# Fused matrix product, bias and tanh by Strassen-Winograd products: the last tanh of a pair written to a tile of the outputs' pool, and the leaving pair reading both m5 sums ahead of m6's products

## The chip, the cores and the metric

The kernel runs on one core of a Trainium2 chip. The metric is the device time of one execution in microseconds; lower is better. The kernel before took 1536.89 us, the median of three runs between 1536.08 and 1539.6 us. The engines are named as in the profile: PE does matrix products (PEld loads its weights beside it), DVE does elementwise work on two operands, ACT does tanh and copies, POOL and SP issue transfers here and compute nothing that matters.

## The reference

```python
def reference(a, b, bias):        # all float32; a, b 4096 x 4096, bias 4096
    return np.tanh(np.matmul(a, b) + bias)
```

## The kernel before

The product is cut in four columns `c` of 1024 output columns (two halves `j` of 512) and, in each, sixteen row pairs of 2 x 128 output rows. One item of work is one pair in one column. An item's 2 x 2 blocks are made by the Strassen-Winograd scheme: seven products `m1` to `m7` in place of eight, each of 16 matmuls of 128x128 weights against 128x512 data in float16. Their left operands are differences of quadrants of `a` (`s1`, `s2`, `s5`, `s6`, `s7`), their right operands sums of blocks of `b` (`d1`, `d3`, `d4`, `e6`, `e7`); DVE makes both. The products are summed in the eight PSUM banks (`ps`) and in float32 tiles: `ds` collects the first output row's left half (and gives the second row's left half on the way), `s` the first row's right half, `o` the second row's right half.

Columns 0 and 1 and the beginnings of columns 2 and 3 are ordinary items or items taken by two. The end of the single items of columns 2 and 3 is done by `four(n)`, which takes two items `p = n` and `q = n + 1` together and does some of their products by the same scheme a second time: `m4`, `m2` and `m3` in every pair, `m6` in all but the leaving one, and `m5` in those that are neither first nor leaving are computed for both items as seven half products of 8 matmuls of 128x256 each, in three groups. `group0` is the half products with left operands `s5` and `s2`, `group1` those with `s1`, `d3` and `d4`, `group2` those with `s7` and `s6`. The small left operands `h` are made by `left(...)` into four places that are used in turn; those right operands (`form`) that are not in SBUF are loaded again, 512 KB each, by POOL whenever a place comes free (`pull_four`). The third sum of a group goes through a copy `x` on ACT (`third`). Column 2 has four such pairs, column 3 has five. The fourth of column 2 is the leaving pair (`leave`), after which the next items are ordinary again; the fifth of column 3 is the last of the program.

The schedule is written by hand: every engine does its instructions in the order in which the code issues them, and tiles of a pool are handed out in turn. Three pools matter. `temps` has two buffers under the name `ds` and two under `sc` (the tile `s`). `outs` has three buffers under the name `o`. A buffer is written again only when the last reader of its earlier tile is done; where that reader is the store to DRAM, when the store has landed.

How a pair ends, and how the next begins, is what the change touches. The function `end` (L933) closes a tile: `tanh` on ACT over the tile itself, and the store by SP (L474) from it. The closing of `ds` and of one set of the tiles `s` is put into the list `left_over`, which the next pair empties a few at a time with `more(4)`, `more(3)`, `more(2)` and `more(1)` (L889) between its own half products, so that these tanhs lie beside `group0` and `group1` of the next pair's `m4` and `m2`. Behind `group2` of `m4` the next pair takes its own two `ds` tiles: `take_d(p)` and `take_d(q)` (L955), DVE additions of the bias to a bank. DVE does after that the operands `s5` and `s2` of the product `x`, which is `m6` in a steady pair. PE meanwhile does `group2` of `m2`, `group0` of `m3`, and then `group0` of `x`, which needs them.

In the leaving pair the order is `m1` of p and q, then for each item: `take("m5", i)` (DVE: two additions, then tanh and store of `s`), the whole product `m6`, `take("m6", i)`, the whole product `m7`, and the end of `ds`.

Of the kernel before, what the change touches and what calls it, by code (L numbers as in the profile page):

```python
# [23 lines left out]
TANH = mybir.ActivationFunctionType.Tanh  # L24
# [87 lines left out]
def kernel(  # L112
# [7 lines left out]
    nc = tc.nc  # L120
# [20 lines left out]
    def tt(out_, in0, in1, op):  # L141
        nc.vector.tensor_tensor(out=out_, in0=in0, in1=in1, op=op)  # L142
# [6 lines left out]
    def bank(n, s, what):  # L149
        two = items[n][2] is not None  # L150
        if what == "w":
            return banks[5 + 2 * (n % 2)]
        if what == "z":
            return banks[4 + 2 * (n % 2) + (s if two else 0)]
        return banks[(0 if what == "d" else 2) + (s if two else n % 2)]
# [158 lines left out]
    def asum(n, name, half=None):  # L314
        s = aset[n]
        x, y = {
            "s2": ("a21", "a22"), "s5": ("a12", "a11"), "s1": ("a22", "a11"),
            "s6": ("a21", "a11"), "s7": ("a22", "a12"),
        }[name]
        over = {"s6": "a21", "s7": "a12"}.get(name)  # L320
        if half == 1:
            pass
        elif name == "s6" and n in partner and by_two(n, "m6"):
            s[name] = side[:, :, ds(NB, NB)].rearrange("p a (b m) -> p a b m", m=P)
            tt(s[name], by_four(s[x]), by_four(s[y]), SUB)
            return
        elif over is None or stays(n):
            s[name] = new_sum([P, T, P], fp16, name, n)
        else:
            s[name] = s[over]  # L330
        ts_ = ds(0, T) if half is None else ds(half * TP, TP)
        tt(s[name][:, ts_], s[x][:, ts_], s[y][:, ts_], SUB)
# [140 lines left out]
    def store(o, pair, r, c, j):  # L473
        nc.sync.dma_start(  # L474
            out=out[ds((2 * pair + r) * P, P), ds(c * NCW + j * NB, NB)], in_=o
        )

    def new_out():
        return outs.tile([P, NB], fp32, name="o", tag="o")

    def result(src, *where):
        o = new_out()
        nc.scalar.activation(o, src, TANH)  # L483
        store(o, *where)
# [361 lines left out]
    def whole(n, left_, right, parts=None, anew=False):  # L846
        at = by_four(aset[n][left_])
        for to, half in parts or ((bank(n, 0, "z"), ds(0, NB)),):
            for t in range(T):
                nc.tensor.matmul(  # L850
                    to[:, half], at[:, t // TB, t % TB], bop[right, t // TB][:, t % TB, half],
                    start=anew and t == 0, stop=t == T - 1, skip_group_check=True,
                )
# [42 lines left out]
    def four(n):  # L896
        c = items[n][0]
        p, q, m = n, n + 1, n + 2
# [5 lines left out]
        pair = {i: items[i][1][0] for i in (p, q)}  # L904
        st = {i: state.setdefault((i, 0), {}) for i in (p, q)}
# [12 lines left out]
        def make(name, i):  # L918
            four_sum(i, name, home[name, i])
# [5 lines left out]
        def step(k):  # L925
            if leave:
                give_back(c, k)

        def one_whole(what, i):
            _, left_, right = next(v for v in PRODUCTS.values() if v[0] == what)  # L930
            whole(i, left_, right, ((bank(i, 0, mine.get(what, "z")), ds(0, NB)),), what in mine)

        def end(name, i, r, j):  # L933
            nc.scalar.activation(st[i][name], st[i][name], TANH)  # L934
            store(st[i][name], pair[i], r, c, j)

        def take(what, i, later=False):
            to = bank(i, 0, mine[what])
            if what == "m6":
                tt(st[i]["o"], st[i]["o"], to, ADD)  # L940
                ready = ("o", i, 1, 1)
            else:
                tt(st[i]["ds"], st[i]["ds"], to, SUB)
                tt(st[i]["s"], to, st[i]["s"], ADD)
                ready = ("s", i, 0, 1)
            if later:
                left_over.append(lambda: end(*ready))
            else:
                end(*ready)

        def take_c(i):
            st[i]["s"] = temps.tile([P, NB], fp32, name="s", tag="sc")
            tt(st[i]["s"], bank(i, 0, "c"), bias_bc[:, NB:], ADD)
# [5 lines left out]
        def take_z(i):  # L959
            st[i]["o"] = new_out()  # L960
            tt(st[i]["o"], st[i]["s"], bank(i, 0, "z"), SUB)
# [104 lines left out]
        if leave:  # L1066
            make("s1", q)
            make("s7", q)
            for i in (p, q):
                take_c(i)  # L1070
            one_whole("m1", p)
            step(12)
            take_z(p)
            one_whole("m1", q)
            take_z(q)
            step(13)
            for i in (p, q):
                take("m5", i)
                one_whole("m6", i)
                step(14 if i == p else 16)  # L1080
                take("m6", i)
                one_whole("m7", i)
                if i == p:
                    asum(m, "s2")
                tt(st[i]["ds"], st[i]["ds"], bank(i, 0, "z"), SUB)
                end("ds", i, 0, 0)
                step(15 if i == p else 17)
            asum(m, "s5")
            for k in range(18, 29):
                at_slot(SLOTS * m + k - 18, give_back, c, k)  # L1090
            return
# [247 lines left out]
    def at_slot(slot, f, *args):  # L1339
        work.setdefault(slot, []).append((f, args))  # L1340
# [403 lines left out]
    for slot in range(1 - len(ORDER), SLOTS * len(items)):  # L1744
        if slot in handed:
            if slot - 1 not in handed:
                c = max(c for c in FOURS if SLOTS * (begins[c] - 2) < slot)
                turn_over(c)
                for n in range(begins[c], ends_with[c], 2):
                    four(n)  # L1750
            continue
        for f, args in work.get(slot, ()):
            f(*args)
        if slot < 0:
            visit(slot + len(ORDER) - 1)
        elif slot == 3:
            last_visit(0)
            last_visit(1)
        for pos, p in PRODUCTS.items():
            n, r = divmod(slot - pos, SLOTS)  # L1760
            if r == 0 and n >= 0 and n not in fours:
                if n < LEAD:
                    product(n, *PRODUCTS[FIRST[pos]])
                elif p[0] not in ("m3", "m4", "m6") or not by_two(n, p[0]):
                    product(n, *p)
        for group in groups.get(slot, ()):
            twice(*group)
# [30 lines left out]
```

## Time and profile before

| | us |
|---|---|
| median of three runs | 1536.89 |
| the profiled execution, whole | 1535.69 |
| its span from the first to the last instruction | 1534.0 |
| PE busy in the span | 1522.5 |
| DVE busy in the span | 1249.9 |
| ACT busy in the span | 336.0 |
| mean granted PE clock | 0.999 |

The time outside the span is 1.69 us. Columns 2 and 3 lie, with their pairs by four, at about 928 to 1113 us and 1303 to 1531 us. In the rows of a timeline the first number is the start and the second the length, both in microseconds; `x16` says how many instructions were merged, and square brackets give how long the engine sat idle before the row and what ended that. A row of a run of PE matmuls is longer than the time until the next can start: sixteen 128x256 matmuls are shown as 1.91 us, and where nothing waits the next run starts 1.75 us after them. So a loss on PE is best read from one start to the next.

### The profile page before, as it was taken

To read this page: it belongs to the slowest core of one execution; us is meant where nothing else is said; L and a number is where in the kernel's file an instruction comes from. 1 tells how busy PE (TensorE), PEld (TensorE's weight loads), DVE (VectorE), ACT (ScalarE), POOL (GpSimd) and SP (SyncE) were. 2 spreads that over 40 slices of the span, in tenths; PEclk is the share of its full clock that TensorE was granted. 3 is DMA by queue.
4 is the path that set the end of the run, shared out by engine and by line. 5 is a ranking of instruction groups with operands and counts; after the bars stand their busy time and mean duration, and the time that the engine had idled before them with its cause. 6 is when DMAs were issued, how large, how long until landed. Compare 5 with 4: busy or idle time off the path is not lost.

```text
span 1534.0 us, 23098 instructions
## 1 busy us (share of the span) xinstructions
PE 1522.5 (99%) x8661; PEld 846.2 (55%) x8661; DVE 1249.9 (81%) x1693; ACT 336.0 (22%) x681; POOL 473.5 (31%) x856
## 2 busy tenths in 40 slices
PE   9999999999999999999999999999999999999999
PEld 4444444444445666544444557767544555777676
DVE  6789877777986876777799878989669977998898
ACT  3432111112221122111122112222122211122222
POOL 8775543334503231344551022111123011211110
PEclk9999999999999999999999999999999999999999
DMA  9999998999969998999997789888978567988874
GB/s 185 180 212 263 279 235 217 221 210 227 204 212 282 273 277 258 248 261 237 207 195 231 259 287 351 291 300 290 323 254 196 178 191 252 340 306 286 297 271 159
DMA packets 209428, 381.41 MB, mean 249 GB/s; under 512 B 25122, under 2 KB 108322, under 8 KB 209316
## 3 DMA queue, kind: packets, MB, share of 16 engines
q0 software_dynamic: 117296, 192.21, 55.6%
q1 hardware_dynamic: 91348, 187.41, 35.9%
q8 instruction: 68, 1.11, 0.3%
q10 hardware_dynamic: 672, 0.33, 0.1%
q14 instruction: 44, 0.36, 0.1%
HBM read 324.01 MB, written 141.56 MB: 304 GB/s over the span
## 4 chain that ended last, share of the span: by engine, by line
PE 97%; DMA 2%; DVE 1%; ACT 0%; issue 0%; ACTq 0%; DVEq 0%
PE ps L463 60%; PE ps L811 14%; PE ps L850 10%; PE ps L638 7%; PE ps L1443 5%; DMA out_dram<-ds 2%; DMA coarse<-in_a_dram 0%; DVE ps L142 0%; DVE h L142 0%; DVE s L142 0%; ACT ds L934 0%; PE warm L1503 0%; ACT x L817 0%; PE spread L426 0%; PE tp L1544 0%
## 5 line engine op out<-in xcount | busy, mean ns | idle before, releaser
L463 PEld LDWEIGHTS <-s 128*128 128x128 f16 x2256 | 220.7, 98 | 260.2 <-DVE s L142 0.2
L463 PEld LDWEIGHTS <-a 128*128 128x128 f16 x1984 | 194.1, 98 | 230.6
L463 PE MATMUL ps<-b,s 128*128 128x512 f16 x1204 | 274.7, 379 | 0.0
L463 PE MATMUL ps<-e,a 128*128 128x512 f16 x964 | 219.6, 379 | 0.0
L463 PE MATMUL ps<-d,a 128*128 128x512 f16 x896 | 202.5, 379 | 0.0
L142 DVE TENSOR_TENSOR s<-a,a 128x2048 f16<-128x2048 f16 (+1 forms) x154 | 185.3, 1206 | 16.6 <-DMA a<-scratch 15.3
L266 DVE STREAM_TRANSPOSE a<-nat 128x1024 f16<-128x1024 f16 (+2 forms) x202 | 175.1, 910 | 9.8 <-PE ps L463 8.3
L811 PEld LDWEIGHTS <-h 128*128 128x128 f16 x1640 | 160.4, 98 | 34.6 <-DVE h L142 8.7
L767 POOL DMA_DIRECT2D form<-form_m x119 | 63.0, 529 | 319.2 <-PE ps L811 284.4
L463 PE MATMUL ps<-d,s 128*128 128x512 f16 x688 | 155.5, 379 | 0.0
L142 DVE TENSOR_TENSOR a<-a,a 128x2048 f16<-128x2048 f16 x118 | 142.6, 1215 | 0.0
L238 POOL DMA_DIRECT2D nat<-in_a_dram x176 | 93.0, 533 | 133.8 <-DVE a L266 65.2
L366 POOL DMA_DIRECT2D b<-in_b_dram x192 | 103.4, 544 | 83.5 <-DVE a L266 31.1
L811 PE MATMUL ps<-form,h 128*128 128x256 f16 x728 | 89.5, 274 | 6.5 <-DVE h L142 6.5
L483 ACT ACTIVATE o<-ps 128x512 f32<-128x512 f32 x92 | 55.2, 600 | 177.0 <-issue 94.6
L142 DVE TENSOR_TENSOR h<-a,a 128x1024 f16<-128x1024 f16 x123 | 82.0, 682 | 0.1
L638 PEld LDWEIGHTS <-h 128*128 128x128 f16 x680 | 66.5, 98 | 16.6
L723 POOL DMA_DIRECT2D form_m<-stage x15 | 8.2, 548 | 199.7 <-DVE stage L142 199.7
L850 PEld LDWEIGHTS <-a 128*128 128x128 f16 x448 | 43.2, 98 | 46.5
L811 PE MATMUL ps<-d,h 128*128 128x256 f16 x576 | 68.8, 273 | 0.0
L142 DVE TENSOR_TENSOR ps<-ps,x 128x256 f32<-128x256 f32 x116 | 49.9, 430 | 20.5 <-PE ps L638 8.7
L142 DVE TENSOR_TENSOR ps<-cs,ps 128x512 f32<-128x512 f32 x43 | 29.5, 693 | 40.9 <-PE ps L463 39.4
(177 smaller groups left out, 1954.9 us busy)
## 6 DMA issues: line engine op xcount, KB each, us to landing
a<-scratch SPq DMA_DIRECT2D x140, 512.0 KB, 5.4
form<-form_m POOLq DMA_DIRECT2D x119, 512.0 KB, 6.1
out_dram<-o SPq DMA_DIRECT2D x207, 256.0 KB, 5.1
nat<-in_a_dram POOLq DMA_DIRECT2D x288, 128.0 KB, 7.1
scratch<-a SPq DMA_DIRECT2D x48, 512.0 KB, 6.6
b<-in_b_dram POOLq DMA_DIRECT2D x160, 128.0 KB, 5.7
scratch<-a SPq DMA_DIRECT2D x32, 256.0 KB, 6.1
cast<-in_b_dram POOLq DMA_DIRECT2D x64, 128.0 KB, 8.9
```

The lines of the kernel that those rows point to most:

```text
L142: nc.vector.tensor_tensor(out=out_, in0=in0, in1=in1, op=op)
L238: nc.gpsimd.dma_start(out=tl[ds(q * QP, QP), :, :], in_=src.rearrange("(mb p) k -> p mb k", p=QP),)
L266: nc.vector.transpose(dst[:, ds(b0 * tb, n * tb), :].rearrange("P (b t) (mb p) -> P mb b t p", t=tb, p=QP), src[:, :, ds(b0, n), :].rearra ...
L366: nc.gpsimd.dma_start(out=dst[ds(q * QP, QP), ds(t, nt)], in_=src)
L463: nc.tensor.matmul(st[where], at, bt, start=(what == "m2" or n < LEAD and what == "m1") and i == 0, stop=i == len(ts_) - 1, skip_group_che ...
L483: nc.scalar.activation(o, src, TANH)
L638: nc.tensor.matmul(to, at, bt, start=False, stop=t == TP - 1, skip_group_check=True)
L723: nc.gpsimd.dma_start(out=forms[what, name], in_=stage)
L767: nc.gpsimd.dma_start(out=rights[what, name], in_=forms[what, name])
L811: nc.tensor.matmul(to, at, bt, start=False, stop=t == TP - 1, skip_group_check=True)
L850: nc.tensor.matmul(to[:, half], at[:, t // TB, t % TB], bop[right, t // TB][:, t % TB, half], start=anew and t == 0, stop=t == T - 1, skip ...
L1443: nc.tensor.matmul(mb[m % 4, j], aq[m, kt // T][:, kt % T, :], right(kt, j), start=fresh and kt == k0, stop=stop and kt == k1 - 1, skip_gr ...
```

## The change

Two things are changed, both in `four`.

First, `end` treats `ds` differently. Before, its tanh wrote over the tile `ds` and the store read it there. Now `result` is called: tanh reads `ds` and writes a new tile `o` of the pool `outs`, and the store reads that. 17 closings are of this kind: two in each of the eight pairs before the last, and one in the last.

Second, in the leaving pair `take("m5", i)` is done for both items ahead of the first `m6` product, where it stood inside the loop for each item.

```diff
         def end(name, i, r, j):
-            nc.scalar.activation(st[i][name], st[i][name], TANH)
-            store(st[i][name], pair[i], r, c, j)
+            if name == "ds":
+                result(st[i][name], pair[i], r, c, j)
+            else:
+                nc.scalar.activation(st[i][name], st[i][name], TANH)
+                store(st[i][name], pair[i], r, c, j)
...
             for i in (p, q):
                 take("m5", i)
+            for i in (p, q):
                 one_whole("m6", i)
                 step(14 if i == p else 16)
                 take("m6", i)
```

The function that is now called was there before:

```python
    def result(src, *where):
        o = new_out()                       # outs.tile(..., tag="o"), three buffers
        nc.scalar.activation(o, src, TANH)
        store(o, *where)
```

The orders of PE and POOL are the same as before. On ACT the closings stand at the same places of a steady pair; their output is another tile. From `more(4)` on in the third pair of column 2, before:

```order
406 L934 ACTIVATE ds<-ds 128x512
407 L817 COPY x<-ps_251 128x256
408 L934 ACTIVATE s<-s 128x512
409 L817 COPY x<-ps_252 128x256
410 L934 ACTIVATE s<-s 128x512
411 L817 COPY x<-ps_249 128x256
412 L934 ACTIVATE ds<-ds 128x512
```

The same place on ACT now:

```order
406 L483 ACTIVATE o<-ds 128x512
407 L817 COPY x<-ps_251 128x256
408 L937 ACTIVATE s<-s 128x512
409 L817 COPY x<-ps_252 128x256
410 L937 ACTIVATE s<-s 128x512
411 L817 COPY x<-ps_249 128x256
412 L483 ACTIVATE o<-ds 128x512
```

Nothing moved there; the first and the last row write `o` in place of `ds`. On DVE the only place that differs is the leaving pair. Its rows from the second `take_z` on, before:

```order
1075 L142 TENSOR_TENSOR o<-s,ps_251 128x512
1076 L142 TENSOR_TENSOR ds<-ds,ps_247 128x512
1077 L142 TENSOR_TENSOR s<-ps_247,s 128x512
1078 L142 TENSOR_TENSOR o<-o,ps_250 128x512
1079 L142 TENSOR_TENSOR s_9842<-a_9608,a_9710 128x2048
1080 L142 TENSOR_TENSOR ds<-ds,ps_254 128x512
1081 L142 TENSOR_TENSOR ds<-ds,ps_253 128x512
1082 L142 TENSOR_TENSOR s<-ps_253,s 128x512
1083 L142 TENSOR_TENSOR o<-o,ps_248 128x512
```

The same rows on DVE now:

```order
1075 L142 TENSOR_TENSOR o<-s,ps_251 128x512
1076 L142 TENSOR_TENSOR ds<-ds,ps_247 128x512
1077 L142 TENSOR_TENSOR s<-ps_247,s 128x512
1078 L142 TENSOR_TENSOR ds<-ds,ps_253 128x512
1079 L142 TENSOR_TENSOR s<-ps_253,s 128x512
1080 L142 TENSOR_TENSOR o<-o,ps_250 128x512
1081 L142 TENSOR_TENSOR s_9852<-a_9614,a_9716 128x2048
1082 L142 TENSOR_TENSOR ds<-ds,ps_254 128x512
1083 L142 TENSOR_TENSOR o<-o,ps_248 128x512
```

The two reads of q's `m5` bank (`ps_253`) stand three rows earlier, ahead of the read of p's `m6` bank (`ps_250`). On SP the store of q's `s` moves with them. The queue in the leaving pair before:

```order
323 L474 DMA out_dram<-s 128x512
324 L603 DMA d_2_6843<-away_m_2_e_6931 128x4x256
325 L603 DMA d_3_6874<-away_m_2_e_6931 128x4x256
326 L474 DMA out_dram<-o 128x512
327 L474 DMA out_dram<-ds 128x512
328 L474 DMA out_dram<-s 128x512
329 L474 DMA out_dram<-o 128x512
330 L474 DMA out_dram<-ds 128x512
```

And now:

```order
321 L474 DMA out_dram<-s 128x512 x2
322 L603 DMA d_2_6843<-away_m_2_e_6931 128x4x256
323 L603 DMA d_3_6874<-away_m_2_e_6931 128x4x256
324 L474 DMA out_dram<-o 128x512 x4
```

Both stores of `s` now stand ahead of the two loads that bring a right operand back (L603).

## The prediction

> **What bounds the kernel now.** I read the page first, then the waits of PE, then the chain of work that ended last, and last the timeline at the places that the chain named.
>
> ```profile
> span 1534.0 us, 23098 instructions
> PE 1522.5 (99%) x8661; PEld 846.2 (55%) x8661; DVE 1249.9 (81%) x1693; ACT 336.0 (22%) x681; POOL 473.5 (31%) x856
> ```
>
> PE is busy for all but 11.5 us, so no change that leaves the products alone can win more than about that and what a lower clock costs. The question is where PE stands still. Its waits, over the whole span:
>
> ```profile
> PE ps L811 <- DVE h L142: 6.5, 3, 2.4
> PE ps L811 <- DVE ps L142: 0.3, 1, 0.3
> ```
>
> Beside the opening these four waits are all. All are in the pairs by four (L811), and DVE is late with an operand `h` or a sum. The chain says why DVE is late:
>
> ```profile
> 1026.47 6.32 DMA out_dram<-ds
> ...
> 1448.01 6.52 DMA out_dram<-ds
> ```
>
> There, and at two places between them, the end of the program hangs on a store of a `ds` tile. The first of the places, in order of time:
>
> ```profile
> 1021.30 0.34 SPq L474 DMA_DIRECT2D out_dram<-ds  x1
> ...
> 1025.81 0.64 ACT L934 ACTIVATE ds<-ds 128x512 f32<-128x512 f32 x1
> 1026.47 0.33 SPq L474 DMA_DIRECT2D out_dram<-ds  x1
> ...
> 1029.68 0.69 DVE L142 TENSOR_TENSOR ds<-ps,bias_bc 128x512 f32<-128x512 f32 x1
> ...
> 1030.38 1.91 PE L811 MATMUL ps<-d,h 128*128 128x256 f16 x16
> ...
> 1032.89 0.69 DVE L142 TENSOR_TENSOR ds<-ps,bias_bc 128x512 f32<-128x512 f32 x1 [2.53 <-DMA out_dram<-ds]
> 1033.50 1.28 DVE L142 TENSOR_TENSOR h<-a 128x1024 f16<-128x1024 f16 x2
> ...
> 1034.24 2.42 PE L811 MATMUL ps<-form,h 128*128 128x256 f16 x16 [1.95 <-DVE h L142]
> ...
> 1036.44 1.91 PE L811 MATMUL ps<-g,h 128*128 128x256 f16 x8
> ...
> 1038.15 2.29 PE L811 MATMUL ps<-g,a 128*128 128x256 f16 x16
> ...
> 1038.66 1.15 ACT L483 ACTIVATE o<-ds 128x512 f32<-128x512 f32 x2
> ...
> 1040.28 1.04 PE L811 MATMUL ps<-form,h 128*128 128x256 f16 x8
> ```
>
> The tanh over q's old `ds` ends at 1026.45, the store leaves at 1026.47 and lands 6.32 us later. `take_d(q)` wants that buffer at about 1030.3, behind `take_d(p)` at 1029.68, and gets it at 1032.89. Behind it on DVE stand the two operands `h` of `m6`, and PE waits for them until 1034.24.
>
> **The release of `ds`.** With the store reading `o`, the old `ds` is free when tanh has read it: 1026.45, nearly 4 us before it is wanted. The wait of 2.53 us then goes whole. What does PE gain? From start to start, less the 1.75 us that sixteen such matmuls take (3.45 us for sixteen of 128x512), in the three other places from these rows:
>
> ```profile
> 1080.32 3.62 PE L850 MATMUL ps<-b,s 128*128 128x512 f16 x16
> 1084.28 1.03 PE L811 MATMUL ps<-g,h 128*128 128x256 f16 x8 [0.34 <-DVE ps L142]
> 1404.96 1.91 PE L811 MATMUL ps<-d,h 128*128 128x256 f16 x16
> 1409.25 1.92 PE L811 MATMUL ps<-form,h 128*128 128x256 f16 x16 [2.38 <-DVE h L142]
> 1451.92 1.91 PE L811 MATMUL ps<-d,h 128*128 128x256 f16 x16
> 1455.98 1.92 PE L811 MATMUL ps<-form,h 128*128 128x256 f16 x16 [2.15 <-DVE h L142]
> ```
>
> The losses are 1034.24 - 1030.38 - 1.75 = 2.11, 1084.28 - 1080.32 - 3.45 = 0.51, 1409.25 - 1404.96 - 1.75 = 2.54 and 1455.98 - 1451.92 - 1.75 = 2.31: together 7.47 us.
>
> What is late next? If nothing waits, `take_d(q)` starts 0.60 us behind `take_d(p)`, at 1030.28, the first `h` 0.60 later and ends at 1031.57. PE is ready for it at 1030.38 + 1.75 = 1032.13 (its weights some 0.1 earlier), so about 0.4 us are left. The second pair of column 3 is a control in the same execution, since there the store was early and DVE waited little:
>
> ```profile
> 1360.55 1.91 PE L811 MATMUL ps<-d,h 128*128 128x256 f16 x16
> ...
> 1360.84 0.69 DVE L142 TENSOR_TENSOR ds<-ps,bias_bc 128x512 f32<-128x512 f32 x1 [0.30 <-DMA out_dram<-ds]
> ...
> 1362.30 1.91 PE L811 MATMUL ps<-form,h 128*128 128x256 f16 x16
> ```
>
> PE goes on after 1362.30 - 1360.55 = 1.75 us, with no loss, though DVE still waited 0.30 us. In the leaving pair its wait is far longer than the loss of 0.51, so that one goes too:
>
> ```profile
> 1081.46 0.69 DVE L142 TENSOR_TENSOR ds<-ps,bias_bc 128x512 f32<-128x512 f32 x1 [1.77 <-DMA out_dram<-ds]
> ```
>
> I take 7.47. The ends: 7.0, if about 0.1 us stays at each place, and 7.6 with the rests in other pairs.
>
> **The clock behind the first gap.** The three runs of matmuls after 1034.24 take 2.20, 1.71 and 2.13 us where 1.75, 0.88 and 1.75 are due: 1.67 us more.
>
> ```profile
> 1036.40:1038.20 1.80, 1.80 (x11) 1.26 (x9) 1.11 (x3) 0.37 (x1) 0.53 (x1) 0.50 0.73 275
> 1409.00:1413.00 4.00, 3.75 (x35) 3.38 (x36) 3.71 (x8) 2.05 (x7) 1.06 (x2) 1.00 0.69 262
> ```
>
> The column behind the five engines is the granted clock: 0.50 behind the first gap, but 1.00 behind the longer one at 1409. The loss of clock in the whole span, 0.1% of 1534 by its mean of 0.999, is about this much, so it happened once and directly behind a gap. With the gap I let it go: 1.67 us, with ends of 0 and 1.67. The Trainium skill, TensorE: Matmul & The Clock Gate, "Why this matters for your kernels", speaks against that: it asks for idle gaps above some 3 us before the clock falls back to half. The gap here was 1.95 us and the clock fell to 0.50 all the same, so the trace does not bear the bound out; by the page the sum would be 7.47 alone.
>
> **The tanh itself.** Seventeen instructions are replaced one for one:
>
> ```profile
> L483 ACT ACTIVATE o<-ds x24: 617/630/633, 916.7 to 1504.5; 128x512 f32<-128x512 f32 x24
> L934 ACT ACTIVATE ds<-ds x17: 629/633/637, 977.6 to 1526.6; 128x512 f32<-128x512 f32 x17
> ```
>
> Out of place costs a median of 630 ns, over itself 633: 17 x 3 ns is nothing, on an engine that is busy for 22%. The stores have the same size and place in SP's queue.
>
> **The pool `outs`.** A steady pair now takes six tiles of three buffers where it took four: old p's `ds`, old q's `ds`, the two results of the second row, the two `o`. So the second result waits for the store of old p's `ds`, and q's `o` for that of old q's `ds`. The nearest store to its user is the former: issued at 1021.30 in the rows above, its buffer wanted by the second of the two tanhs that start at 1038.66, at 1039.2, 17 us on. The longest landing of such a store and the only wait of this kind in column 2:
>
> ```profile
> DMA to landing us min/median/max: 2.0/4.0/9.8
> ACT o L483 <- DMA out_dram<-o: 1.8, 1, 1.8
> ```
>
> Seven microseconds are left over the worst, so I put 0. Bounds: 0, since an `o` buffer frees no one earlier, and a cost of 1.8 us, if one such wait fell ahead of a copy that PE needs.
>
> **The leaving pair.** The two additions for q's `m5` now stand ahead of the read of p's `m6`:
>
> ```profile
> 1102.24 1.36 SPq L603 DMA_DIRECT2D d<-away_m_e  x2
> 1102.66 0.69 DVE L142 TENSOR_TENSOR o<-o,ps 128x512 f32<-128x512 f32 x1 [1.51 <-PE ps L850]
> ...
> 1109.37 3.62 PE L850 MATMUL ps<-e,a 128*128 128x512 f16 x16
> ...
> 1112.82 1.03 PE L463 MATMUL ps<-side,s 128*128 128x512 f16 x4
> ```
>
> They take 2 x 0.60 us and find 1.51 us in which DVE waited for PE, so the read of `m6` starts when it did. Without that cover it would be 1.2 us late, and even that reaches no product, as the next user, at 1112.82, is 10 us away. q's tanh of `s`, 0.63 us, runs at about 1102.4, ahead of p's `o`, in idle time of ACT. On SP the two loads of `d` (L603) now stand behind q's store: about 1.2 us later, at 1103.4. They fill the last two blocks of `d4`, which the next items, in their first halves, don't read. POOL's queue is as it was. PE has no gap from 1109.37 to 1112.82 (3.45 us), so there is nothing to win either: 0, with 0.5 us to either side.
>
> **The sum.** 7.47 + 1.67 = 9.14 us. Against the profiled execution: 1535.69 - 9.14 = 1526.55. The median of the runs is 1.20 us above that execution; with the same offset it is 1527.75, and I say 1527.8, 0.6% less. The likeliest case alone spans 1526.3 (offset gone too) to 1529.0.
>
> **The rivals.**
>
> *The clock loss is not the gap's.* Two gaps out of three, both longer, were followed by a clock of 1.00; something else may have set it off and will again. Then 7.47 is all: 1536.89 - 7.47 = 1529.4, between 1528.2 and 1530.5. This is what the page's bound would give.
>
> *The next thing late is a `form`, and the time is longer than before.* PE comes to `m6` 2 to 4 us sooner, but the loads of its right operands are issued when `m2`'s products free their places, as before.
>
> ```profile
> 1029.96 0.53 POOL L767 DMA_DIRECT2D form<-form_m  x1 [2.09 <-PE ps L811]
> ...
> DMA to landing us min/median/max: 3.4/6.1/6.8
> ```
>
> The fifth of the seven, `d4`, goes out at 1029.96 and lands 6.1 us later, at 1036.1. Its half product is the third of the run that stood at 1040.28 and comes 2.11 + 1.67 sooner: 1036.50 + 2 x 0.875 = 1038.25. So 2.1 us are left, and by the longest landing 1.4. Each microsecond beyond that costs PE one in each of the seven pairs that load for `m6`. A landing of 8.2 + 9.14/7 = 9.5 us is the point from which the time is longer than before; with 10.5 it would be 1536.89 + 7 x 1.0 = 1543.9. Nothing in the pair comes near 9.5, and the control pair runs under the same loads.
>
> *The change only moves the wait.* A store still holds a buffer, now one of three; if ACT or DVE waited for it as long as `take_d(q)` did, the gaps would stand a few rows later and the time would be 1536 to 1537. Against it speak the 17 us above; for it, only that a pair now takes six tiles.
>
> **How the numbers follow.** The likeliest case 0.60; the clock loss of another cause 0.22; a late `form`, or an operand that leaves part of the gaps, 0.05 with a gain of 3 to 5 us (1532 to 1534) and 0.05 slower; the wait only moved 0.06; anything else 0.02, slower. A measurement can tell 0.2%, that is 3.07 us, from no change. Faster: 0.60 + 0.22 + 0.05 = 0.87; the same: 0.06; slower: 0.07. The first two cases hold 0.82, so the range reaches over them, with the bounds of the unknown costs (0.5 below for the rests, 1.8 above for one wait): 1525.5 to 1531.5.
>
> **What would show it.** Right: no wait of DVE's `ds` rows for a store by `ds`; PE without a wait by L811 but for tenths; 1.75 us between the two starts at each of the three places; the granted clock 1.00 through 1000 to 1100; the chain without its four pieces of DMA; DVE in the leaving pair doing `ds`, `s`, `ds`, `s` in a row. Wrong: a wait of `o` rows for stores of `o` in a pair by four, PE waiting for a DMA into `form`, or a clock below 1 without a gap ahead of it.

## The result, and the profile after

The changed kernel takes 1527.72 us, the median of six runs between 1527.12 and 1528.5. The kernel before takes 1539.14 us (six runs, 1536.08 to 1539.6; three of them are the runs whose median of 1536.89 us the prediction starts from). The ratio is 0.9931, with a 95% interval of 0.9918 to 0.9943: 11.4 us, or 0.7%, are won, where 9.1 us were forecast. The profiled execution took 1527.72 us as a whole. The page of the profile after:

```profile
span 1526.0 us, 23094 instructions
PE 1520.6 (100%) x8661; PEld 846.2 (55%) x8661; DVE 1250.0 (82%) x1693; ACT 336.5 (22%) x681; POOL 475.1 (31%) x856
```

All the waits of PE in the span (engine, line, what was waited for; us in total, times, longest):

```profile
PE warm L1507 <- DVE idle L401: 1.3, 1, 1.3
PE ps L1447 <- DVE oa L266: 0.6, 1, 0.6
PE tp L1548 <- DVE first L1543: 0.6, 1, 0.6
```

All three belong to the opening. The two rows of L811, 6.5 and 0.3 us before, are gone. The place of the first gap, the third pair of column 2, in the timeline after:

```profile
1030.88 1.28 DVE L142 TENSOR_TENSOR ds<-ps,bias_bc 128x512 f32<-128x512 f32 x2
...
1031.58 1.91 PE L811 MATMUL ps<-d,h 128*128 128x256 f16 x16
...
1032.08 1.28 DVE L142 TENSOR_TENSOR h<-a 128x1024 f16<-128x1024 f16 x2
...
1033.33 1.91 PE L811 MATMUL ps<-form,h 128*128 128x256 f16 x16
...
1035.08 1.04 PE L811 MATMUL ps<-g,h 128*128 128x256 f16 x8
...
1035.95 1.91 PE L811 MATMUL ps<-g,a 128*128 128x256 f16 x16
...
1037.69 1.04 PE L811 MATMUL ps<-form,h 128*128 128x256 f16 x8
```

`take_d(p)` and `take_d(q)` are one row now, with nothing waited for between them. PE's next start is 1033.33 - 1031.58 = 1.75 us on (at the other two places 1403.61 - 1401.87 = 1.74 and 1448.02 - 1446.27 = 1.75), and the three runs behind it take 1.75, 0.87 and 1.74 us, where they took 2.20, 1.71 and 2.13. In the chain that ended last the stretches of the pairs by four are whole (start, length, what):

```profile
1019.49 22.73 PE ps L811 x208
...
1389.78 22.73 PE ps L811 x208
...
1434.18 22.73 PE ps L811 x208
```

Each of these was broken by a piece of DMA before. The fourth gap, in the leaving pair, is gone too: the next run starts 1081.19 - 1077.73 = 3.46 us on, and 3.45 are due.

```profile
1077.73 3.62 PE L850 MATMUL ps<-b,s 128*128 128x512 f16 x16
...
1081.19 1.04 PE L811 MATMUL ps<-g,h 128*128 128x256 f16 x8
```

The same pair, around the reads that were moved:

```profile
1097.97 0.68 DVE L142 TENSOR_TENSOR ds<-ds,ps 128x512 f32<-128x512 f32 x1
...
1098.57 0.68 DVE L142 TENSOR_TENSOR s<-ps,s 128x512 f32<-128x512 f32 x1
...
1099.57 0.69 DVE L142 TENSOR_TENSOR o<-o,ps 128x512 f32<-128x512 f32 x1 [0.32 <-PE ps L850]
```

The two additions for q have filled 1.2 of the 1.51 us in which DVE waited for `m6`; 0.32 us are left.

### The profile page after: what moved, and what is told of

Its sections match the earlier page's. It is cut to its first block, busy times and chain, and to the rows that moved or that the text cites. A ratio compares the mean times of both kernels' runs of the same rounds, so it can differ in the third digit from the quotient of the medians.

```text
span 1526.0 us, 23094 instructions
## 1 busy us (share of the span) xinstructions
PE 1520.6 (100%) x8661; PEld 846.2 (55%) x8661; DVE 1250.0 (82%) x1693; ACT 336.5 (22%) x681; POOL 475.1 (31%) x856
## 4 chain that ended last, share of the span: by engine, by line
PE 92%; DMA 4%; POOL 2%; DVE 1%; issue 1%; ACT 0%; SPq 0%; DVEq 0%; POOLq 0%; ACTq 0%
PE ps L463 58%; PE ps L811 16%; PE ps L850 10%; PE ps L638 7%; DMA b<-in_b_dram 2%; DMA a<-scratch 1%; POOL b L366 1%; POOL land L1488 1%; DMA land<-in_a_dram 1%; DMA form<-g 1%; PE ps L1447 0%; POOL side L1536 0%; DVE s L142 0%; DVE d L142 0%; DVE oa L266 0%
## 5 line engine op out<-in xcount | busy, mean ns | idle before, releaser
L142 DVE TENSOR_TENSOR s<-a,a 128x2048 f16<-128x2048 f16 (+1 forms) x154 | 185.4, 1206 | 15.9 <-DMA a<-scratch 14.6
L811 PEld LDWEIGHTS <-h 128*128 128x128 f16 x1640 | 160.2, 98 | 25.9 <-DVE h L142 0.6
L811 PE MATMUL ps<-form,h 128*128 128x256 f16 x728 | 89.0, 273 | 0.0
L811 PE MATMUL ps<-d,h 128*128 128x256 f16 x576 | 68.8, 273 | 0.0
```

The costliest lines, as they stand in the source:

```text
L811: nc.tensor.matmul(to, at, bt, start=False, stop=t == TP - 1, skip_group_check=True)
```

## The experiments

Each kernel is given as a short diff against the kernel before or the changed one. The kernel before was run beside them; its runs lay between 1535.74 and 1543.75 us in the first group (median 1538.75, 23 runs) and between 1536.24 and 1541.87 in the second (median 1539.55, 15 runs).

**The tanh alone.** The changed kernel with the second part undone:

```diff
             for i in (p, q):
                 take("m5", i)
-            for i in (p, q):
                 one_whole("m6", i)
```

> The changed kernel without its second part: the leaving pair reads m5 of q after m7 of p again, the closings of ds still write o. Theory (the release of ds is all of the gain): no wait of a ds row for a store, PE without a gap in the pairs by four, 1527 to 1528.5 us like the whole change. Rival (the second part carries the 2 us by which the gain of 11.4 us is larger than the sum of 9.1): 1529 to 1530 us.

It took 1527.52 us (1526.77 to 1527.78; ratio to before 0.9922, 0.991 to 0.9934), as fast as the whole change. The first part is all of the gain. One wait in its profile is of a kind that the whole change did not show:

```profile
PE ps L811 <- DMA form<-form_m: 0.4, 1, 0.4
```

PE did wait once for a right operand, in the first pair of column 2, for 0.4 us.

**The read-out alone.** The kernel before with the second part:

```diff
             for i in (p, q):
                 take("m5", i)
+            for i in (p, q):
                 one_whole("m6", i)
```

> The kernel before with the second part alone: the leaving pair reads both m5 sums ahead of m6's products, tanh of ds still over ds. Theory: PE had no gap there, so the time of the kernel before, 1536 to 1540 us, with the same four waits of ds rows for stores (10.8 us in all) and the same PE gaps (2.1, 0.5, 2.5 and 2.3 us). Rival (the second part is worth 2 us): 1534 to 1538 us.

It took 1539.43 us (1536.99 to 1541.4; ratio 1.0002, 0.9994 to 1.0011): no difference. The four gaps, in the timeline of PE:

```profile
1034.92 1.92 PE L811 MATMUL ps<-form,h 128*128 128x256 f16 x16 [2.07 <-DVE h L142]
1083.92 1.03 PE L811 MATMUL ps<-g,h 128*128 128x256 f16 x8 [0.97 <-DVE ps L142]
...
1410.09 3.59 PE L811 MATMUL ps<-form,h 128*128 128x256 f16 x16 [3.58 <-DVE h L142]
1459.54 3.03 PE L811 MATMUL ps<-form,h 128*128 128x256 f16 x16 [2.10 <-DVE h L142]
```

They stand where they stood, but not with the same lengths: 8.72 us in all where the execution on which the prediction rests had 6.82. The third is 3.58 us long where it was 2.38, and DVE's wait for the store at that place is longer too, 4.16 us where it was 2.96:

```profile
1408.74 0.69 DVE L142 TENSOR_TENSOR ds<-ps,bias_bc 128x512 f32<-128x512 f32 x1 [4.16 <-DMA out_dram<-ds]
```

The landing of the stores decides the length of a gap, and it varies from one execution to the next.

**Only q's tile.** The changed kernel, with p's `ds` closed as before:

```diff
-            if name == "ds":
+            if name == "ds" and i == q:
                 result(st[i][name], pair[i], r, c, j)
```

> The changed kernel, but only q's ds is closed through a tile o; p's tanh goes over ds as before. Theory: p's store leaves some 4 us earlier and was never the one that PE hung on, so this has the whole gain but tenths: 1527 to 1529 us, no PE gap at the three places. Rival (both releases count, or six tiles of three buffers matter): between the two kernels, 1530 to 1535 us.

It took 1528.35 us (1527.39 to 1529.8; ratio 0.9927, 0.9914 to 0.9939). The time is as expected, the reason not wholly. The three gaps are gone, but there are two others, in the second pairs of columns 2 and 3:

```profile
988.53 0.69 DVE L142 TENSOR_TENSOR ds<-ps,bias_bc 128x512 f32<-128x512 f32 x1 [2.46 <-DMA out_dram<-ds]
...
989.88 1.92 PE L811 MATMUL ps<-form,h 128*128 128x256 f16 x16 [1.88 <-DVE h L142]
```

The other, at 1361.27, is 0.93 us long. After the first pair of a column `left_over` holds q's closing ahead of p's. A buffer that comes free first is handed out first, so there `take_d(p)` gets q's old buffer and `take_d(q)` gets p's: the row that waits is the second of the two, and the first, at 985.39, waited for no store. The store of p issued at 979.45 took 9.1 us to land. So the expectation that p's store "was never the one that PE hung on" does not hold: the store that counts is that of the `ds` that is closed last.

**Only p's tile.** The counterpart, with `i == p` in the same line.

> The counterpart: only p's ds goes through o; q's tanh goes over ds and its store reads ds. Theory: take_d(q) still waits for q's store at three places of steady pairs and in the leaving pair, so nothing is won: 1536 to 1540 us, PE gaps of 2.1 to 2.5 us as before. Rival as for only q: between the two kernels.

It took 1538.43 us (1536.55 to 1540.83; ratio 0.9997, 0.9989 to 1.0006): nothing won. Its gaps on PE:

```profile
1035.29 1.92 PE L811 MATMUL ps<-form,h 128*128 128x256 f16 x16 [2.15 <-DVE h L142]
1084.32 1.03 PE L811 MATMUL ps<-g,h 128*128 128x256 f16 x8 [1.00 <-DVE ps L142]
...
1409.48 3.38 PE L811 MATMUL ps<-form,h 128*128 128x256 f16 x16 [2.58 <-DVE h L142]
1458.08 1.92 PE L811 MATMUL ps<-form,h 128*128 128x256 f16 x16 [2.35 <-DVE h L142]
```

With the last kernel this places the gain: it hangs on the one tile whose tanh comes last.

**No new tile, the store earlier.** The kernel before, with q's closing moved ahead of the two of `s`:

```diff
-        left_over.append(lambda: end("ds", q, 0, 0))
+        left_over.insert(2, lambda: end("ds", q, 0, 0))
```

> The kernel before with no new tile at all: q's ds is closed (tanh over ds, store from ds) directly behind p's, ahead of the two closings of s, in the pairs that follow a steady one. The store then leaves at about 1022.8 in place of 1026.5 and lands, by 6.5 us, at 1029.3, about 1 us before take_d(q) wants the buffer. Theory (only the moment at which q's old ds comes free counts): the wait goes or shrinks to under 0.5 us, PE has no gap over 0.2 us in the steady pairs, 1527 to 1529.5 us. Rival (the tile in the outputs' pool itself matters, or the store's landing stretches so that the wait stays): 1533 to 1539 us.

It took 1528.74 us (1527.0 to 1531.42; ratio 0.9932, 0.9918 to 0.9945). So the gain does not need the pool or the tile `o`; it needs the buffer to come free early enough. The third pair of column 2 in its timeline:

```profile
1023.39 1.80 SPq L474 DMA_DIRECT2D out_dram<-ds  x2
...
1024.20 0.63 ACT L934 ACTIVATE ds<-ds 128x512 f32<-128x512 f32 x1
...
1031.76 1.28 DVE L142 TENSOR_TENSOR ds<-ps,bias_bc 128x512 f32<-128x512 f32 x2
...
1032.46 1.91 PE L811 MATMUL ps<-d,h 128*128 128x256 f16 x16
...
1034.21 1.91 PE L811 MATMUL ps<-form,h 128*128 128x256 f16 x16
```

The last tanh ends at 1024.83 and its store has landed by 1032.4, so that DVE waits for nothing and PE starts 1.75 us on. The margin is thin: in the whole stretch two `ds` rows still waited, 1.2 us in all, PE waited 0.3 us for an `h` behind one of them, and the runs spread over 4.4 us where those of the change spread over 1.4.

**DVE late without a store.** Three kernels from the changed one repeat the addition of `take_d(p)` at the three places of the gaps, 2, 5 and 8 times:

```diff
             take_d(i)
+            if i == p and n in (begins[2] + 4, begins[3] + 4, begins[3] + 6):
+                for _ in range(2):          # 5, 8
+                    tt(st[p]["ds"], bank(p, 0, "d"), bias_bc[:, :NB], ADD)
```

> The changed kernel with DVE made late without any wait for a transfer: take_d(p) is done twice more (the same values again) at the three places that had a gap, the third pair of column 2 and the third and fourth of column 3. Two additions of 0.60 us less 0.4 us that are free make a PE gap of about 0.8 us at each. Theory: 3 x 0.8 = 2.4 us, and no loss of clock if that hangs on the length of the gap: 1530 us. If any gap costs the clock 1.67 us each time: 1535 us.

> The same with five additions more: PE gaps of about 2.6 us, as long as before the change, with no store to wait for. Theory (a gap of this length costs its length, and in some executions 1.67 us of clock behind it, whatever made it): 1527.7 + 7.8 = 1535.5 us without a clock loss, and runs that lie 1.7, 3.3 or 5.0 us above that, up to 1540.5; a granted clock of 0.5 behind a gap where the run is longer. Rival (the upper runs of the kernel before had another cause, transfers or stores): all runs within 1 us of 1535.5 and a clock of 1.00.

> The same with eight additions more: PE gaps of about 4.4 us. Theory: 3 x 4.4 = 13.2 us, and if the loss of clock comes surely behind a longer gap, 3 x 1.67 = 5.0 us more in every run: 1546 us. If it comes by chance as behind the gaps of 2 to 2.5 us: runs spread between 1541 and 1546 us in steps of 1.7. With no loss at all: 1541 us.

They took 1529.87 us (1529.18 to 1530.54), 1541.62 us (1538.24 to 1543.06) and 1550.55 us (1548.4 to 1552.38). The first gap of each, by two, five and eight:

```profile
1034.23 1.92 PE L811 MATMUL ps<-form,h 128*128 128x256 f16 x16 [0.78 <-DVE h L142]
```

```profile
1035.42 3.20 PE L811 MATMUL ps<-form,h 128*128 128x256 f16 x16 [2.96 <-DVE h L142]
```

```profile
1038.04 3.60 PE L811 MATMUL ps<-form,h 128*128 128x256 f16 x16 [5.13 <-DVE h L142]
```

And the 8 us behind each of the three gaps, in the view of stretches (busy time of PE, PEld, DVE, ACT and POOL, then the granted clock, the DMA share and GB/s), by two (the first gap alone), five and eight:

```profile
1034.23:1042.23 8.00, 8.00 (x74) 7.16 (x75) 7.68 (x14) 3.05 (x8) 2.64 (x5) 1.00 0.95 353
```

```profile
1035.42:1043.42 8.00, 8.00 (x58) 6.54 (x59) 6.40 (x12) 2.88 (x8) 1.58 (x3) 0.79 0.64 228
1410.85:1418.85 8.00, 8.00 (x58) 6.56 (x59) 6.43 (x12) 2.88 (x8) 1.58 (x3) 0.79 0.61 209
1460.05:1468.05 8.00, 8.00 (x47) 6.09 (x48) 5.35 (x11) 2.51 (x7) 1.06 (x2) 0.63 0.59 205
```

```profile
1038.04:1046.04 8.00, 8.00 (x55) 6.41 (x56) 6.01 (x12) 2.78 (x8) 1.32 (x3) 0.74 0.51 171
1415.65:1423.65 8.00, 8.00 (x50) 6.15 (x50) 5.57 (x11) 2.50 (x7) 1.06 (x2) 0.66 0.47 158
1468.00:1476.00 8.00, 8.00 (x55) 6.29 (x56) 6.01 (x12) 2.74 (x8) 1.27 (x3) 0.73 0.49 156
```

The clock column is 1.00 behind all three gaps of 0.78 us, and the mean clock of each of the five runs is 1.000; the column is below 1 behind all gaps of 2.95, 2.96 and 5.13 us. With five additions the three gaps are 8.9 us, each 0.16 us more from start to start, 9.4 us; 1541.62 - 1527.72 = 13.9, so 4.5 us are lost beside them. The clock column gives 8 x (0.21 + 0.21 + 0.37) = 6.3 us for the profiled execution, in which 1542.70 - 1527.72 - 9.4 = 5.6 us are lost. With eight the gaps are 15.9 us of 22.8, and 6.9 us are lost beside them; the column gives 8 x (0.26 + 0.34 + 0.27) = 7.0 for the profiled execution, in which 6.3 are lost. So the column accounts for the loss to within 0.7 us. No transfer had to be waited for here. A gap is enough, whatever made it, and the rival, that the clock had another cause, falls for gaps of 3 us and more. Both medians lie above what was expected, 1540.5 us at most and 1546 us, for two reasons. The estimate for the lengths was low: the addition repeated over the same tile takes (2.96 - 0.78) / 3 = 0.73 us, and not 0.60. And behind a gap of 3 us or more the clock cost up to 3.0 us, not 1.67 each time.

## Why the prediction was right

**The release of `ds`.** Right in place and mechanism. The wait of `take_d(q)` was for the store of the tile closed last, and it goes whole. The control pair had shown the outcome: 1.75 us from start to start, as at all three places now (1.75, 1.74 and 1.75). That early closing gives the same time without the new tile shows that the release is the cause and not the pool.

**Its size.** The working can be tested between two marks that both profiles have: the first stretch of the pairs by four, and the last run of the program, in the chain. Before:

```profile
928.42 22.92 PE ps L811 x208
...
1527.63 3.51 PE ps L850 x32
```

After:

```profile
929.82 22.83 PE ps L811 x208
...
1519.67 3.51 PE ps L850 x32
```

That is 599.21 us before and 589.85 after: 9.36 us, against the 9.14 of the sum. So the sum was right for the execution from which it was made. The changed execution came to the first mark 1.40 us later, so that between the two profiled executions only 7.97 us show. The opening, which neither part of the change touches, varies by as much: in the ten profiled executions the first run of L811 starts between 928.25 us (the kernel before) and 929.65 us (the change), and the tanh alone, which has the same new tile, comes to it at 928.57.

**The time of 1527.8 us.** That it agrees with the measured 1527.72 us to 0.1 us is luck. The sum gave 1526.55 us for the profiled execution, and the prediction added 1.20 us, by which the median of three runs of the kernel before lay above that execution. But the change takes away the gaps that make those runs differ, so nothing showed that this offset would stay. It happened to make up for the later opening of the changed execution (1527.72 - 1526.55 = 1.17 us).

**What the sum left out.** The medians of six runs differ by 11.4 us, 2.3 more than forecast. With three more runs the median of the kernel before went from 1536.89 to 1539.14 us, by 2.25. The profiled execution, at 1535.69 us, lay below all six, and its gaps were short: 6.82 us where the read-out alone and p's tile alone, two kernels that take as long as the one before, had 8.72 and 8.08. The leaving pair's gap was 0.97 and 1.00 us in these two and 0.34 in the execution the sum was made from. So the terms that were mis-sized are "7.47" and "1.67": they are true of one execution, and other executions lose more. The two kinds of loss account for the others as well. Between the same two marks the read-out alone takes 1532.72 - 928.99 = 603.73 us and p's tile alone 1529.59 - 929.03 = 600.56, 13.9 and 10.7 us more than the change. Their gaps are 9.4 and 8.7 us from start to start, and their lost clock, by the column over the 8 us behind each gap, is 4.6 and 1.7: 14.0 and 10.4. Beside the 9.14 of the sum, the read-out alone lost 1.9 us more to gaps and 2.9 more to the clock, p's tile alone 1.2 more to gaps only. Of the 38 runs of the kernel before that stood beside the experiments, 7 had a mean clock of 1.000 to three places; their median is 1538.06, still 10.3 us above the change. The other 31 have means from 0.995 to 0.999 and reach up to 1543.75. So both terms vary from run to run. How the 2.3 us are divided between longer gaps, more lost clock and the opening wasn't taken apart.

**The clock.** Right to let it go with the gap, and the rival at 0.22 is out: no run of the change, of the tanh alone, of q alone, of the early closing or of the short gaps had a mean below 1.000. What was wrong is to take the loss as a fixed 1.67 us: it depends on how many gaps of an execution are followed by a lower clock. The prediction set the trace against a rule of the Trainium skill (TensorE: Matmul & The Clock Gate, "Why this matters for your kernels"), by which a gap has to exceed some 3 us. The rows go with the order of size in it, not with the bound: gaps of 1.95, 2.10 and 2.58 us cost the clock, those of 2.07, 2.15, 2.35 and 2.38 did not, and those of 2.95 us and more always did.

**The pool `outs`.** Right: after the change no row of `ds` or `o` waits for a store between 935 and 1110 us or from 1300 us on, where all the pairs by four but the beginning of the first lie, and early closing without the pool is no faster. The two waits of ACT for a store of `o` that are left, 1.69 us at 920.46 and 4.97 us at 1292.83, lie ahead of the pairs by four and were there before (1.83 and 5.01 us).

**The leaving pair.** Right: no difference either way (1.0002 with it alone, 1527.52 against 1527.72 without it), and the 0.3 us that the working left on DVE was measured as 0.32.

**A late `form`.** Right for the pair that was worked out: `d4`, issued at 1031.17, landed after 5.4 us, at 1036.6, and its half product runs from 1038.57 + 0.875 = 1039.4, with 2.9 us to spare. But the wait exists: 0.4 us for the tanh alone and 0.5 for early closing, at 940.62 and 941.55 in the first pair of column 2.

## What to carry to other kernels

A tile that is computed in place and then stored belongs to the store until that has landed, some 6 to 9 us here, and not to the engine that finished it; if the tile comes from a small pool that the critical engine needs soon, either let the last operation write to a tile with more time to spare, or do that operation earlier in the queue. Look for the one tile that is closed last, since the others had time. And read a gap on PE from start to start and with the clock behind it: here a gap of 2 to 3 us was in some executions followed by a loss of another 1.7 to 3.0 us. Before forecasting, see how much the gaps vary between executions: the profile from which this forecast was made had short gaps, and the forecast gain was 2.3 us too small.

## What was not expected of the hardware

The loss of clock depends on the length of the gap with a band of chance. Gaps by the profiled executions: none of those of 0.78 (three), 0.93, 0.97, 1.00 and 1.88 us was followed by a clock below 1.00; of the eight between 1.95 and 2.58 us (1.95, 2.07, 2.10, 2.15 twice, 2.35, 2.38 and 2.58) three were, 1.95, 2.10 and 2.58; all of 2.95, 2.96 (two), 3.58 and 5.13 us (three) were. Behind the short ones the loss is 8 x 0.21 = 1.7 us in 8 us, behind the longer ones 1.7 to 3.0. Rows of this kind, the 8 us behind the gaps of 1.95 and 2.38 us (before), of 3.58 and 2.10 us (the read-out alone) and of 2.58 us (p's tile alone):

```profile
1034.24:1042.24 8.00, 8.00 (x58) 6.54 (x59) 6.55 (x12) 2.88 (x8) 1.58 (x3) 0.79 0.79 283
1409.25:1417.25 8.00, 8.00 (x74) 7.18 (x75) 7.68 (x14) 3.06 (x8) 2.65 (x5) 1.00 0.82 292
```

```profile
1410.09:1418.09 8.00, 8.00 (x48) 6.00 (x49) 5.45 (x11) 2.51 (x7) 1.06 (x2) 0.64 0.55 181
1459.54:1467.54 8.00, 8.00 (x58) 6.56 (x59) 6.55 (x12) 2.88 (x8) 1.59 (x3) 0.79 0.72 263
```

```profile
1409.48:1417.48 8.00, 8.00 (x58) 6.55 (x59) 6.22 (x12) 3.07 (x8) 1.58 (x3) 0.79 0.71 258
```

What decides within the band is not shown by these runs.

The landing of a store of 256 KB from one queue and of one size varied from 2.4 us (issued at 1021.30, before) over 6.3 us (1026.47) to 9.1 us (979.45, q's tile alone), within 50 us of the same stage. PE hung on the second and the third, not on the first. All stores to the output between 915 and 1110 us took 2.0 to 9.6 us before and 2.0 to 10.6 with early closing; a margin against such a store has to be counted by the longest.
